# A hybrid encoder layer on one core: the passage to the MLP regrouped by PSUM bank, the residual's squares moved to the units, and the first gate's steps set further apart

## The chip, the core and the metric

The kernel runs on one core of a Trainium2 chip. The metric is the device time of one launch in microseconds (us); several runs are made and their median counts. A profiled execution leaves a trace of every instruction. The engines are named as the profile names them: PE (TensorE matmul), PEld (its weight loads), DVE (VectorE), ACT (ScalarE), POOL (GpSimd) and SP (SyncE, which here only issues DMAs). Each engine works through its own instructions in order and waits on semaphores for the others.

## The reference

One layer of an encoder block on 256 tokens of width 2048, all float32. Three mixers read one projection; the RWKV branch ends in a group norm times a gate. Cut to what matters here:

```
def reference(x, ...):
    mix = hybrid_mixer(_rms_norm(x, norm_mix_pre), w_in, ...)   # 3 branches, gates, w_out
    x = x + _rms_norm(mix, norm_mix_post)
    hdn = jnp.square(jax.nn.relu(_rms_norm(x, norm_mlp_pre) @ w_mlp_up))
    x = x + _rms_norm(hdn @ w_mlp_down, norm_mlp_post)

def rwkv7_time_mix(z, ...):
    ...
    y = ((y - mean) * lax.rsqrt(var + RWKV_GN_EPS) * ln_w + ln_b)
    y = y + jnp.sum(r_h * k_h * r_k, axis=-1, keepdims=True) * v_h
    return y * g                                  # g = sigmoid(gd) @ g_up
```

## The kernel before

Every matrix product runs on PE with operands split in two float32r parts, a high part `hi` (a rounded copy) and a low part `lo = x - hi`. Of weights, which stream from memory in tiles of 128x1024 through three buffers (`raw`, loaded by SP's queue in `wraw`, L145), ACT makes the high part `whi` (L152) and DVE the low part `wlo` (L153). Activations are kept as `pk` tiles of 128x512, the high part in the first half, the low part in the second; `split` (L229 to L234) makes them: ACT writes the high part (L233 with a scale), DVE subtracts (L234). `unit` and `up` then multiply eight `pk` tiles with one weight tile: eight matmuls of 512 columns with `whi` (L168, the last one L176) and eight of 256 columns with `wlo` (L172). A unit is two such halves.

PE's order in the first part of the program (mixers, branches) is written out by hand: `gemm` and `tok` (L214, L198) call `tick` after every few matmuls, which adds their estimated time to a clock, and threads of mixer work (generators that yield "how many us later to go on") put their small steps between the matmuls when their due time has come. `gate_norm` is such a thread, once for each half of the RWKV heads (`hf` 0 and 1). For each of four head pairs `p` it multiplies `y` by the inverse deviation `ri` (DVE, L773), applies weight and bias (ACT, L774), adds the bonus (DVE, L775), computes the gate on PE (L779 and L780, from two small weights `gup` that are loaded one pair ahead by `gup_load`: a POOL memset L751 and two DMAs from ACT's queue, L752 and L753) and multiplies (DVE, L781). The gates' results, like all results of mixer steps, lie in four PSUM banks in turn (`mps`); a bank is free when its reader is done. The `yield` of 7.5 us ahead of the loop and of 2.0 us in it set how far PE's gate matmuls lie apart.

From the last group of the output product on, the order is no longer by hand: a scheduler orders each engine's instructions from its own cost estimates and the order in the code. There the passage to the MLP stands. For each half of the tokens, `tt`, the sum of squares is finished (ACT, L969), `rstd_of` turns it into an inverse root in two POOL instructions on 128x1 (L939, L940), and `add_mixed` (DVE, L956) adds the normed mix to the residual `x1[tt]` (in the trace's rows `x`; in the order's rows `x_1333` for `tt` 0, `x_1334` for `tt` 1). PE transposes it, four blocks of 128x128 into one `mps` bank (L988: blocks `k2` and `k2+1`, both token halves), and the two blocks of a bank are split to the `pk` tiles that feed the MLP's units. ACT and DVE never read one bank at the same time: semaphores keep their reads of a bank apart.

In the first eight units ACT also sums the squares of the residual, 512 columns each time (L1113 in `up`'s `post`); its output tile `junk` is thrown away, only the sum in `ss3` is used, by L1117 to L1120, and from there at the very end. The scheduler may place these squares as early as the residual is there. The residual's copy to memory (`xs`, L1261 and L1262) stands in SP's queue ahead of the next weight loads. The layer ends with `rstd_of` again, once for each token half, and the last additions (L1352).

Of the kernel before, what the change touches and what calls it, by code (L numbers as in the profile page):

```python
# [10 lines left out]
F32 = mybir.dt.float32  # L11
F32R = mybir.dt.float32r
AF = mybir.ActivationFunctionType
ALU = mybir.AluOpType
# [3 lines left out]
T = 256  # L18
D = 2048
# [31 lines left out]
def hybrid_block(ctx, tc, xt, x, gains, params, consts, lora, gup, wst, out):  # L51
    nc = tc.nc
    V, A, G, PE = nc.vector, nc.scalar, nc.gpsimd, nc.tensor
# [21 lines left out]
    def pk():  # L75
        return pkpool.tile([128, 512], F32R, tag="pk", name=nm("pk"), bufs=24)
# [14 lines left out]
    def P(name, i=0, r=slice(0, 128)):  # L91
        return par[r, PC[name] + i:PC[name] + i + 1]
# [134 lines left out]
    def split(src, dst, scale=None):  # L227

        if scale is None:  # L229
            A.activation(dst[:, 0:T], src, AF.Copy)  # L230
            V.tensor_tensor(dst[:, T:], src, dst[:, 0:T].bitcast(F32), ALU.subtract)
        else:
            A.activation(dst[:, 0:T], src, AF.Copy, scale=scale)  # L233
            V.scalar_tensor_tensor(dst[:, T:], src, scale, dst[:, 0:T].bitcast(F32), ALU.mult, ALU.subtract)  # L234
# [64 lines left out]
    for h in range(2):  # L299
        w = {}  # L300
        for k in range(8 * h, 8 * h + 8):
            xsplit(k)
            i = k - 8 * h
            if i in (0, 3, 5):
                j = len(w)
# [36 lines left out]
    for h in range(8):  # L342
        ps = qb[h] if h < 3 else unit(xpk)
# [400 lines left out]
    def gate_norm(hf, y, bon, sy, sz):  # L744
        PR = range(4 * hf, 4 * hf + 4)
        gqs = {}

        def gup_load(p):
            if p in PR:
                gqs[p] = gq = rp.tile([128, 2, 128], F32, tag="gup", name=nm("gup"), bufs=2)  # L750
                G.memset(gq[:, 1, :], 0.0)  # L751
                nc.scalar.dma_start(out=gq[:, 0, :], in_=gup[0:128, 128 * p:128 * p + 128])  # L752
                nc.scalar.dma_start(out=gq[0:32, 1, :], in_=gup[128:160, 128 * p:128 * p + 128])  # L753

        gup_load(PR[0])
        var = rp.tile([128, 4, T], F32, tag="XT", name=nm("gn"), bufs=2)
        ri = rp.tile([128, 4, T], F32, tag="XT", name=nm("gn"), bufs=2)
        sc = rp.tile([128, 4, T], F32, tag="Ti", name=nm("gn"), bufs=1)
        for i, p in enumerate(PR):
            A.activation(sc[:, i, :], y[p], AF.Square)  # L760
            if i % 2:
                yield 1.6
        for i2 in range(2):
            ps = mps()
            for i in range(2):
                PE.matmul(ps[:, i * T:i * T + T], C("bones"), sc[:, 2 * i2 + i, :], start=True, stop=True)
            A.activation(var[:, 2 * i2:2 * i2 + 2], ps.rearrange("p (a b) -> p a b", a=2), AF.Identity, scale=1.0 / 64,
                         bias=cst[:, 1:2])
        yield 2.0
        rsqrt(ri, var, sc)  # L770
        yield 7.5
        for i, p in enumerate(PR):
            V.tensor_tensor(y[p], y[p], ri[:, i, :], ALU.mult)  # L773
            A.activation(y[p], y[p], AF.Identity, scale=P("lnw", p), bias=P("lnb", p))  # L774
            V.tensor_tensor(y[p], y[p], bon[p], ALU.add)  # L775
            gup_load(p + 1)
            gq = gqs[p]
            ps = mps()
            PE.matmul(ps[:, 0:T], gq[:, 0, :], sy, start=True, stop=False)  # L779
            PE.matmul(ps[:, 0:T], gq[:, 1, :], sz, start=False, stop=True)  # L780
            V.tensor_tensor(y[p], ps[:, 0:T], y[p], ALU.mult)  # L781
            yc[p] = y[p]
            yield 2.0
        mark(f"gn{hf}")

    def mixers():
# [41 lines left out]
    for s in ("q", "k"):  # L828
        lst = []
        for h in range(4):  # L830
            ps = unit(upk)
# [11 lines left out]
    for hf in range(2):  # L843
        for s, mo in (("k", MU_K), ("r", MU_R), ("v", MU_V)):
            for p in range(4 * hf, 4 * hf + 4):
                ps = unit(upk)
# [84 lines left out]
    def rstd_of(ss, eps, sums):  # L931

        if sums is None:
            sums = cpool.tile([128, 1], F32, name=nm("ssum"))
            V.tensor_reduce(sums, ss[:, 0:3], AX.X, ALU.add)
            V.tensor_scalar(sums, sums, 1.0 / D, eps, ALU.mult, ALU.add)
            return sums
        r = cpool.tile([128, 1], F32, name=nm("rs"))
        G.tensor_scalar(r, ss[:, 3:4], 1.0 / D, sums, ALU.mult, ALU.add)  # L939
        G.tensor_tensor(r, r, cst[:, 2:3], ALU.pow)  # L940
        return r

    g2, loads = gain(0, [fm().rearrange("p a b -> p (a b)")[:, 0:512] for _ in range(4)])
    x1 = [p2.tile([128, D], F32, tag="x1", name=nm("x1"), bufs=2) for _ in range(2)]
# [7 lines left out]
    def junk():  # L952
        return p2.tile([128, 512], F32, tag="junk", name=nm("junk"), bufs=2)
# [30 lines left out]
    trs = []  # L984
# [6 lines left out]
    for k2 in range(0, KT, 2):  # L991
        while len(trs) < min(k2 // 2 + 4, 8):
            trs.append(mps())
            turned(2 * len(trs) - 2, 0)
        if k2 == 8:
            pend()
        add_mixed(1, 128 * k2, 256)
        turned(k2, 1)
        for i in range(2):
            u = pk()  # L1000
            split(trs[k2 // 2][:, i * T:i * T + T], u, P("g3", k2 + i))
            upk2.append(u)

# [79 lines left out]
    def up(j):  # L1085
# [10 lines left out]
        def post():  # L1096
# [13 lines left out]
            h = hid[j // 2]  # L1110
            A.activation(h[:, 0:4:3] if j % 2 == 0 else h[:, 1:3], t.rearrange("p (s t) -> p s t", s=2), AF.Square)
            if j < 8:
                A.activation(junk(), x1[j % 2][:, 512 * (j // 2):512 * (j // 2) + 512], AF.Square,  # L1113
                             accum_out=ss3[:, j % 2, j // 2:j // 2 + 1])
            if j in (8, 9):
                e = cpool.tile([128, 2], F32, name=nm("eps4"))
# [362 lines left out]
```

## Time and profile before

| | us |
|---|---|
| median of 3 runs | 1534.03 (1532.95 to 1536.06) |
| profiled execution, its own time | 1534.53 |
| its span, first to last instruction | 1532.8 |
| PE busy in it | 1503.2 |
| DVE, ACT, POOL busy | 1192.7, 917.8, 91.0 |

The profiled execution lies 0.50 us above the median. Rows of the timeline read: start, duration, engine, line, operation, output and input tiles, number of instructions merged, and in brackets how long the engine sat idle before and what released it. In rows by stretches of time, each engine's busy time with its instructions in brackets is followed by the granted TensorE clock (1.00 is full), the DMA engines' busy share and GB/s. A matmul's duration contains its passage through the array; the distance from one start to the next is what it costs on a busy PE.

### The profile page before, as it was taken

The page shows a single profiled execution, that of the slowest core. Times are in us where ns is not written, and L with a number is a line of the kernel's source. Part 1 is how long each engine was busy: PE and PEld are TensorE (multiplying, and loading weights), DVE is VectorE, ACT ScalarE, POOL GpSimd, SP SyncE. Part 2 cuts the span into 40 slices and gives each one's busy share as a digit, 9 for nine tenths or more (in the row PEclk, how much of TensorE's full clock was granted, in tenths as well). Part 3 has the DMA queues.
Part 4 walks back from the last instruction along what each step waited for, and adds up shares of the span by engine and source line. Part 5 has one row for each costly group of instructions (what it writes and reads, how often), then busy time and mean ns, then how long its engine had stood idle before and what let it go on. Part 6 is the DMA issues. An engine that isn't in the chain of part 4 may idle for free.

```text
span 1532.8 us, 22383 instructions
## 1 busy us (share of the span) xinstructions
PE 1503.2 (98%) x8294; PEld 1262.6 (82%) x8294; DVE 1192.7 (78%) x1608; ACT 917.8 (60%) x1340; POOL 91.0 (6%) x163
## 2 busy tenths in 40 slices
PE   7999999999999999999999999999999999999997
PEld 6888888888777788778888788888888888888885
DVE  6865567789548789447755868989899999899986
ACT  6664566554546553555444767777667776676753
POOL 0021000000000100000000000000000000000000
PEclk9999999999999999999999999999999999999998
DMA  7555445445534445535695657888888888888974
GB/s 259 192 166 166 164 165 181 165 150 183 182 111 150 165 152 184 175 124 179 208 322 187 231 181 222 249 263 239 262 253 258 242 254 270 249 246 264 260 247 151
DMA packets 105117, 316.88 MB, mean 207 GB/s; under 512 B 10288, under 2 KB 12720, under 8 KB 104624
## 3 DMA queue, kind: packets, MB, share of 16 engines
q1 hardware_dynamic: 93536, 282.76, 54.1%
q0 software_dynamic: 8064, 29.36, 10.3%
q10 hardware_dynamic: 3408, 3.34, 0.6%
q8 instruction: 65, 1.06, 0.3%
q14 instruction: 44, 0.36, 0.1%
HBM read 281.86 MB, written 4.19 MB: 187 GB/s over the span
## 4 chain that ended last, share of the span: by engine, by line
PE 53%; DVE 1%; DMA 1%; ACT 1%; issue 0%; POOL 0%; DVEq 0%; POOLq 0%; ACTq 0%
PE gps L168 14%; PE gps L214 10%; PE gps L172 8%; PE mps L1209 3%; PE mps L1210 3%; PE mps L1211 3%; PE gps L198 3%; PE gps L1211 2%; PE gps L1209 2%; PE gps L1210 2%; PE gps L176 1%; DMA sp<-in_wst_dram 1%; DVE x L1352 0%; DVE wlo L153 0%; ACT junk L1113 0%
## 5 line engine op out<-in xcount | busy, mean ns | idle before, releaser
L153 DVE TENSOR_TENSOR wlo<-raw,whi 128x1024 fp32r<-128x1024 f32 x507 | 616.0, 1222 | 192.2 <-ACT whi L152 174.8
L152 ACT ACTIVATE whi<-raw 128x1024 fp32r<-128x1024 f32 x507 | 533.9, 1057 | 276.0 <-PE gps L214 107.7
L168 PE MATMUL gps<-pk,whi 128*128 128x512 f32 x1301 | 330.9, 393 | 0.1
L214 PE MATMUL gps<-whi,pk 128*128 128x512 f32 x1144 | 291.5, 394 | 0.0
L168 PEld LDWEIGHTS gps<-pk,whi 128*128 128x128 f32 x1301 | 241.1, 188 | 48.4 <-issue 0.9
L214 PEld LDWEIGHTS gps<-whi,pk 128*128 128x128 f32 x1144 | 213.7, 188 | 45.8 <-issue 1.0
L172 PEld LDWEIGHTS gps<-pk,wlo 128*128 128x128 f32 x1391 | 190.1, 190 | 14.6 <-issue 1.2
L172 PE MATMUL gps<-pk,wlo 128*128 128x256 f32 x1391 | 195.8, 283 | 0.0
L214 PE MATMUL gps<-wlo,pk 128*128 128x512 f32 x572 | 157.4, 394 | 0.0
L214 PEld LDWEIGHTS gps<-wlo,pk 128*128 128x128 f32 x572 | 106.9, 188 | 23.2 <-issue 0.7
L1075 DVE TENSOR_TENSOR sp<-raw,sp 128x1024 fp32r<-128x1024 f32 x67 | 81.7, 1220 | 4.8 <-ACT sp L1074 4.6
L1074 ACT ACTIVATE sp<-raw 128x1024 fp32r<-128x1024 f32 x67 | 70.7, 1055 | 14.9 <-PE mps L1211 3.9
L1101 ACT ACTIVATE sp<-gps 128x512 f32<-128x512 f32 x52 | 31.1, 597 | 80.7 <-PE gps L176 80.7
L198 PE MATMUL gps<-whi,pk 128*128 128x512 f32 x264 | 71.9, 393 | 0.0
L1209 PE MATMUL mps<-whi,fm 128*128 128x512 f32 x168 | 66.2, 394 | 0.0
L1210 PE MATMUL mps<-whi,fm 128*128 128x512 f32 x168 | 65.8, 392 | 0.0
L1211 PE MATMUL mps<-wlo,fm 128*128 128x512 f32 x168 | 65.5, 390 | 0.0
L1171 POOL DMA_DIRECT2D raw<-raw x40 | 35.0, 874 | 430.8 <-DVE raw L1168 133.4
L198 PEld LDWEIGHTS gps<-whi,pk 128*128 128x128 f32 x264 | 49.3, 188 | 10.6 <-ACT whi L152 0.2
L1211 PE MATMUL gps<-wlo,fm 128*128 128x512 f32 x126 | 49.3, 391 | 0.4 <-DVE wlo L153 0.4
L1209 PE MATMUL gps<-whi,fm 128*128 128x512 f32 x126 | 49.2, 391 | 0.0
L1168 DVE TENSOR_TENSOR raw<-raw,raw 128x1024 f32<-128x1024 f32 x40 | 48.8, 1219 | 0.4
(342 smaller groups left out, 1961.4 us busy)
## 6 DMA issues: line engine op xcount, KB each, us to landing
raw<-in_wst_dram SPq DMA_DIRECT2D x502, 512.0 KB, 4.4
raw<-raw POOLq DMA_DIRECT2D x40, 512.0 KB, 7.3
sp<-in_wst_dram SPq DMA_DIRECT2D x16, 512.0 KB, 5.6
raw<-sp POOLq DMA_DIRECT2D x8, 512.0 KB, 7.7
sp<-raw POOLq DMA_DIRECT2D x8, 512.0 KB, 6.5
x<-in_x_dram SPq DMA_DIRECT2D x8, 256.0 KB, 6.3
xs<-x SPq DMA_DIRECT2D x2, 1024.0 KB, 4.0
x<-xs SPq DMA_DIRECT2D x4, 512.0 KB, 7.4
```

The source lines that it names most:

```text
L152: A.activation(hi, raw, AF.Copy)
L153: V.tensor_tensor(lo, raw, hi.bitcast(F32), ALU.subtract)
L168: PE.matmul(ps, hi[:, i * 128:i * 128 + 128], pks[i], start=first and i == 0, stop=False)
L172: PE.matmul(ps[:, 0:T], lo[:, i * 128:i * 128 + 128], pks[i][:, 0:T], start=False, stop=False)
L198: PE.matmul(ps[tt], pks[k][:, c:c + 128], w[:, (k - k0) * 512:(k - k0) * 512 + 512], start=k == 0 and part == 0 and w is hl[0], stop=w is ...
L214: PE.matmul(ps[tt], pks[k][:, c:c + 128], w[:, (k - k0) * 512:(k - k0) * 512 + 512], start=k == 0 and part == 0 and w is hl[0], stop=False)
L1074: A.activation(hi, raw, AF.Copy)
L1075: V.tensor_tensor(lo, raw, hi.bitcast(F32), ALU.subtract)
L1168: V.tensor_tensor(x, x, z, ALU.add)
L1209: PE.matmul(Q[f], p, w, start=d == 0 and i == 0, stop=False)
L1210: PE.matmul(Q[f], pl, w, start=False, stop=False)
L1211: PE.matmul(Q[f], p, wl, start=False, stop=d == nd - 1 and i == 1)
```

## The change

Four things. The first half's gate waits 11.5 us instead of 7.5 ahead of its loop and 2.8 instead of 2.0 between pairs. The first of the two small instructions of `rstd_of` moves from POOL to DVE (four instructions in all: two in the passage, two at the end). In the passage the two high parts of a bank are written first and then its two low parts. The residual's squares write their useless output over the unit's own PSUM bank `ps[0]` instead of `junk`, so that each can run only after its unit.

```
-        yield 7.5
+        yield 7.5 if hf else 11.5
         for i, p in enumerate(PR):
             ...
-            yield 2.0
+            yield 2.0 if hf else 2.8
...
-        G.tensor_scalar(r, ss[:, 3:4], 1.0 / D, sums, ALU.mult, ALU.add)
+        V.tensor_scalar(r, ss[:, 3:4], 1.0 / D, sums, ALU.mult, ALU.add)
         G.tensor_tensor(r, r, cst[:, 2:3], ALU.pow)
...
-        for i in range(2):
-            u = pk()
-            split(trs[k2 // 2][:, i * T:i * T + T], u, P("g3", k2 + i))
-            upk2.append(u)
+        src = [trs[k2 // 2][:, i * T:i * T + T] for i in range(2)]
+        us = [pk(), pk()]
+        for i, u in enumerate(us):
+            A.activation(u[:, 0:T], src[i], AF.Copy, scale=P("g3", k2 + i))
+        for i, u in enumerate(us):
+            V.scalar_tensor_tensor(u[:, T:], src[i], P("g3", k2 + i), u[:, 0:T].bitcast(F32), ALU.mult, ALU.subtract)
+        upk2.extend(us)
...
-                A.activation(junk(), x1[j % 2][:, 512 * (j // 2):512 * (j // 2) + 512], AF.Square,
+                A.activation(ps[0], x1[j % 2][:, 512 * (j // 2):512 * (j // 2) + 512], AF.Square,
```

In the changed kernel the lines behind the passage lie three lower (L1113 becomes L1116), and the high and low parts of the passage are L1002 and L1004. The engines' orders differ from before in three places only.

**The first gate.** PE ahead of the third head pair's gate (L779, L780), before; `gps` are the two banks of the weight product that runs meanwhile, L567 and L569 belong to the second half's mixer:

```order
L214 MATMUL gps_4486<-wlo_4558,pk_293 128x512
L214 MATMUL gps_4487<-wlo_4558,pk_293 128x512
L567 MATMUL mps_4616<-zx,lor_4416 128x256
L569 MATMUL mps_4618<-zx,lor_4416 128x256
L214 MATMUL gps_4486<-wlo_4558,pk_294 128x512
L779 MATMUL mps_4643<-zy,gup_4598 128x256
L780 MATMUL mps_4643<-zz,gup_4598 128x256
L214 MATMUL gps_4487<-wlo_4558,pk_294 128x512
```

and now (the weight tiles have other numbers):

```order
L214 MATMUL gps_4487<-whi_4628,pk_298 128x512 x2
L214 MATMUL gps_4486<-wlo_4629,pk_297 128x512
L214 MATMUL gps_4487<-wlo_4629,pk_297 128x512
L214 MATMUL gps_4486<-wlo_4629,pk_298 128x512
L779 MATMUL mps_4690<-zy,gup_4645 128x256
L780 MATMUL mps_4690<-zz,gup_4645 128x256
L214 MATMUL gps_4487<-wlo_4629,pk_298 128x512
```

The third gate now follows 24 more matmuls than before, in the second weight tile after the one with `wlo_4558`; the first gate stands about where the third did, and the fourth 13 matmuls behind the third. ACT's queue at that place, before and now, with the loads of `gup` in it:

```order
L152 ACTIVATE whi_4589<-raw_4587 128x1024
L752 DMA gup_4598<-in_gup_dram 128x128
L753 DMA gup_4598<-in_gup_dram 32x128
L152 ACTIVATE whi_4650<-raw_4648 128x1024
L774 ACTIVATE g_772_3978<-g_772_3978,par 128x256
L752 DMA gup_4639<-in_gup_dram 128x128
L753 DMA gup_4639<-in_gup_dram 32x128
```

```order
L752 DMA gup_4645<-in_gup_dram 128x128
L774 ACTIVATE g_772_3978<-g_772_3978,par 128x256
L576 ACTIVATE lw_4611<-mps_4605,wah 128x256
L577 ACTIVATE tha_4613<-mps_4607,wah 128x256
L578 ACTIVATE lw_4611<-lw_4611,cst 128x256
L774 ACTIVATE g_773_3979<-g_773_3979,par 128x256
L753 DMA gup_4645<-in_gup_dram 32x128
L582 ACTIVATE ep_4615<-cs_4612 128x4x64
L583 ACTIVATE em_4614<-cs_4612 128x256
L587 ACTIVATE g_887_4655<-tha_4613,oka,wah 128x256
L774 ACTIVATE g_774_3980<-g_774_3980,par 128x256
L752 DMA gup_4686<-in_gup_dram 128x128
```

Before, all loads of the third and fourth pair stood ahead of the second L774; now the second load of the third pair stands behind the second L774, and both of the fourth pair behind the third. On DVE one more weight split stands ahead of the first L781.

**The passage.** DVE from the second token half on, before (`pk_7701` and `pk_7704` are the two blocks of the first bank, `mg` the mix):

```order
L956 SCALAR_TENSOR_TENSOR x_1334_7021<-mg_7023,rs_7682,x_1334_7021 128x256 x4
L234 SCALAR_TENSOR_TENSOR pk_7701<-mps_7686,par,pk_7701 128x256
L967 TENSOR_TENSOR mg_7023<-gps_7525,fm_7019 128x512
L956 SCALAR_TENSOR_TENSOR x_1334_7021<-mg_7023,rs_7682,x_1334_7021 128x256
L234 SCALAR_TENSOR_TENSOR pk_7704<-mps_7686,par,pk_7704 128x256
L234 SCALAR_TENSOR_TENSOR pk_7713<-mps_7689,par,pk_7713 128x256
L956 SCALAR_TENSOR_TENSOR x_1334_7021<-mg_7023,rs_7682,x_1334_7021 128x256 x3
```

and now, from the ninth low part on:

```order
L1004 SCALAR_TENSOR_TENSOR pk_7750<-mps_7707,par,pk_7750 128x256
L1004 SCALAR_TENSOR_TENSOR pk_7751<-mps_7707,par,pk_7751 128x256
L956 SCALAR_TENSOR_TENSOR x_1334_7021<-mg_7023,rs_7682,x_1334_7021 128x256 x3
L153 TENSOR_TENSOR wlo_7791<-raw_7788,whi_7790 128x1024
L1004 SCALAR_TENSOR_TENSOR pk_7759<-mps_7719,par,pk_7759 128x256
```

Now L939, L967 and five additions come first, ten low parts follow without a break, then three additions, one weight split and the six remaining low parts. Before, five weight splits (one of them L1075), one sum of weights and the eight small instructions L1117 to L1120 stood among the sixteen low parts. ACT, before:

```order
L1113 ACTIVATE junk_7863,ss_7685<-x_1333_7020 128x512
L233 ACTIVATE pk_7701<-mps_7686,par 128x256
L1113 ACTIVATE junk_7916,ss_7685<-x_1334_7021 128x512
L1113 ACTIVATE junk_7980,ss_7685<-x_1333_7020 128x512
L233 ACTIVATE pk_7704<-mps_7686,par 128x256
L233 ACTIVATE pk_7713<-mps_7689,par 128x256
```

Now the sixteen high parts stand together with one weight tile among them, and each square in its unit, as here in the first one:

```order
L1108 ACTIVATE tmp_7857<-gps_7794 128x256
L152 ACTIVATE whi_7866<-raw_7864 128x1024
L1110 ACTIVATE tmp_7856<-tmp_7856 128x256
L1116 ACTIVATE gps_7794,ss_7685<-x_1333_7020 128x512
L1114 ACTIVATE pk_7861<-tmp_7856 128x2x128
L152 ACTIVATE whi_7888<-raw_7886 128x1024
```

The first load into the space that the residual leaves (`sp`, L1064 in SP's queue) moves 17 places back, and its split (L1074, L1075) out of the passage.

**The end.** DVE's last instructions, before and now (`y_8487` and `y_8479` are the second token half, `pk_13653` and `pk_13645` the gain):

```order
L1341 TENSOR_TENSOR y_8486<-y_8486,pk_13653 128x512
L1352 SCALAR_TENSOR_TENSOR x_2587_13828<-y_8486,rs_13975,x_2587_13828 128x512 x4
L1337 TENSOR_TENSOR y_8487<-y_8487,gps_13923 128x512
L1341 TENSOR_TENSOR y_8487<-y_8487,pk_13653 128x512
L1352 SCALAR_TENSOR_TENSOR x_2588_13829<-y_8487,rs_14008,x_2588_13829 128x512 x4
```

```order
L1355 SCALAR_TENSOR_TENSOR x_2579_13820<-y_8478,rs_13967,x_2579_13820 128x512 x4
L1340 TENSOR_TENSOR y_8479<-y_8479,gps_13915 128x512
L939 TENSOR_SCALAR rs_14000<-ss_7785,ssum_13911 128x1
L1344 TENSOR_TENSOR y_8479<-y_8479,pk_13645 128x512
L1355 SCALAR_TENSOR_TENSOR x_2580_13821<-y_8479,rs_14000,x_2580_13821 128x512 x4
```

L939 has moved here from POOL, ahead of the multiplication by the gain.

## Prediction

> **What bounds the kernel now.** I read the page's head first, then PE's waits, then the clock by stretches.
>
> ```profile
> span 1532.8 us, 22383 instructions
> PE 1503.2 (98%) x8294; PEld 1262.6 (82%) x8294; DVE 1192.7 (78%) x1608; ACT 917.8 (60%) x1340; POOL 91.0 (6%) x163
> PE gps L310 <- ACT whi L152: 8.9, 1, 8.9
> PE mps L988 <- DVE x L956: 2.1, 2, 1.8
> PE mps L779 <- DVE g L781: 2.0, 1, 2.0
> ```
>
> PE bounds: 29.6 us of the span are left to it, and its waits lie at the start (8.9 us, untouched by the change), in the passage (L988) and at one gate matmul (L779). Everything else can only pay where it shortens one of these or the end, after PE's last matmul. But a wait costs more than its length, as the granted clock (first number behind POOL) shows:
>
> ```profile
> 478.00:482.64 4.64, 2.65 (x12) 1.43 (x10) 4.64 (x10) 2.01 (x3) 1.35 (x3) 1.00 0.40 128
> 482.64:486.38 3.74, 3.74 (x10) 2.94 (x10) 3.74 (x7) 2.95 (x7) 0.20 (x1) 0.54 0.70 248
> 841.40:844.98 3.58, 1.44 (x9) 0.84 (x8) 2.86 (x6) 2.02 (x5) 1.41 (x2) 0.97 0.50 195
> 844.98:848.29 3.31, 2.99 (x10) 1.85 (x10) 3.10 (x8) 2.58 (x8) 0.00 (x0) 0.52 0.60 248
> 848.29:857.52 9.23, 7.91 (x47) 6.11 (x47) 8.59 (x23) 7.94 (x21) 0.00 (x0) 1.00 0.67 246
> 890.00:1310.00 420.00, 420.00 (x2170) 360.27 (x2170) 380.64 (x447) 296.12 (x400) 33.01 (x38) 1.00 0.82 244
> ```
>
> After each of the two long waits the clock stands at about half for some 3.4 us. From 890 us on PE is full for 420 us, so what is won earlier is carried to the end.
>
> **The gate.** Its rows, with two full units of matmuls from later on as a measure of the rate, and the loads of `gup`:
>
> ```profile
> 480.15 0.50 PE L214 MATMUL gps<-wlo,pk 128*128 128x512 f32 x1
> 480.37 1.22 DVE L153 TENSOR_TENSOR wlo<-raw,whi 128x1024 fp32r<-128x1024 f32 x1
> 481.84 0.42 DVE L773 TENSOR_TENSOR g<-g,gn 128x256 f32<-128x256 f32 x1
> 482.17 0.42 DVE L781 TENSOR_TENSOR g<-mps,g 128x256 f32<-128x256 f32 x1
> 482.29 0.60 ACT L774 ACTIVATE g<-g,par 128x256 f32<-128x256 f32 x1 [0.20 <-DVE g L773]
> 482.64 0.95 PE L779 MATMUL mps<-zy,gup 128*128 128x256 f32 x2 [1.99 <-DVE g L781]
> 868.53 2.00 PE L168 MATMUL gps<-pk,whi 128*128 128x512 f32 x8
> 870.37 1.12 PE L172 MATMUL gps<-pk,wlo 128*128 128x256 f32 x8
> 871.32 1.78 PE L168 MATMUL gps<-pk,whi 128*128 128x512 f32 x7
> DMA to landing us min/median/max: 1.5/2.2/4.2
> ```
>
> At full clock eight matmuls of 512 columns take 870.37 - 868.53 = 1.84 us, 0.23 each, eight of 256 take 0.95, 0.12 each. The third gate needs the bank that the first one's L781 frees. PE's last matmul ahead of it was issued by 480.15 + 0.23 = 480.38; it stood until 482.64, 2.26 us, and lost 3.74 x (1 - 0.54) = 1.7 us to the clock: 4.0 us in all. Now 24 more matmuls stand ahead of the third gate, so PE comes to it at 480.4 + 24 x 0.23 = 485.9. On DVE one split more (1.22) stands ahead of the first L781: 482.17 + 1.22 + 0.42 = 483.8. The bank is free 2.1 us early: the wait goes, and the clock with it does not fall.
>
> What is late next is a load. The second load of the third gate's weight is queued on ACT behind the second L774, which follows its L773 (now 481.84 + 1.22 = 483.06) by 482.29 - 481.84 = 0.45: issued at 483.5, landed after the median of 2.2 us at 485.7, after the longest at 487.7. It is wanted by L780, two matmuls into the gate, at 486.3. The fourth gate comes 13 matmuls (3.0 us) and a gate (four matmuls, 0.9 us at most) later, at 489.8; its loads stand behind the third L774, behind which I count a split, a scan and three ACT steps after the first L781, about 487.2: landed at 489.4, or 491.4. Both fit at the median and miss by 1.4 to 1.6 us at the worst. Such a miss leaves 2.4 of the 4.0, and if the clock falls once more (1.7) 0.7. Bounds -4.0 to +0.5 (a wait of the old kind and length once more); I take -3.8, since both medians fit.
>
> [...]
>
> **The passage.** Its rows:
>
> ```profile
> 842.91 0.86 POOL L939 TENSOR_SCALAR rs<-ss,ssum 128x1 f32<-128x1 f32 x1 [1.97 <-ACT junk L969]
> 840.98 2.74 DVE L956 SCALAR_TENSOR_TENSOR x<-mg,rs,x 128x512 f32<-128x512 f32 x4 [0.21 <-POOL rs L940]
> 843.85 0.56 POOL L940 TENSOR_TENSOR rs<-rs,cst 128x1 f32<-128x1 f32 x1
> 844.44 1.67 DVE L956 SCALAR_TENSOR_TENSOR x<-mg,rs,x 128x256 f32<-128x256 f32 x4 [0.72 <-POOL rs L940]
> 845.71 0.47 ACT L233 ACTIVATE pk<-mps,par 128x256 fp32r<-128x256 f32 x1 [2.29 <-PE mps L988]
> 849.77 0.87 DVE L234 SCALAR_TENSOR_TENSOR pk<-mps,par,pk 128x256 fp32r<-128x256 f32 x2
> 863.21 0.48 DVE L234 SCALAR_TENSOR_TENSOR pk<-mps,par,pk 128x256 fp32r<-128x256 f32 x1 [0.40 <-ACT pk L233]
> 851.84 2.26 SPq L145 DMA_DIRECT2D raw<-in_wst_dram  x2
> 876.31 1.04 ACT L152 ACTIVATE whi<-raw 128x1024 fp32r<-128x1024 f32 x1
> 879.71 2.00 PE L168 MATMUL gps<-pk,whi 128*128 128x512 f32 x8
> raw<-in_wst_dram SPq DMA_DIRECT2D x502, 512.0 KB, 4.4
> L152 ACT ACTIVATE whi<-raw 128x1024 fp32r<-128x1024 f32 x507 | 533.9, 1057 | 276.0 <-PE gps L214 107.7
> L1113 ACT ACTIVATE junk<-x x8: 616/630/650, 842.7 to 851.9; 128x512 f32<-128x512 f32 x8
> L1113 ACT ACTIVATION_READ_ACCUMULATOR junk<-x x8: 188/200/219, 843.2 to 852.4; 128x1 f32 x8
> ```
>
> L939 on DVE wins nothing here. For the second half it now queues behind the four additions that end at 840.98 + 2.74 = 843.72, takes 0.20 (L936 below), and POOL's L940 starts at 843.9 against 843.85. For the first half a weight split hides it. L967 fills the wait.
>
> From 844.5 DVE runs: five additions 0.40 apart (1.67 less one of 0.48, over three) to 846.5, ten low parts as far apart (0.87 less 0.48) to 850.5, three additions to 851.7, one split (1.2) to 852.9, six low parts, the last begun at 854.9 and done by 855.4; before, that one ended at 863.69. ACT loses eight squares, 8 x (0.63 + 0.20) = 6.6 us, and stays ahead of DVE: from 845.71 sixteen high parts of 0.47 and one weight tile of 1.06 end by 854.3 at the latest. PE then: fifteenth block ready 855.0, eight low matmuls, unit 0 done 856.4; the low weights of unit 1 are split by 852.9 + 2.4 + 1.2 = 856.5; two lots of 0.95, seven matmuls of 0.23 and one more give 860.3; unit 2 takes 2 x (1.84 + 0.95) = 5.6, to 865.9, against 868.53 before. The half clock falls on the first blocks again, since PE still stands until 844.98 and then waits for the first low part: the four matmuls of the first two blocks that fall into it lose 0.23 each, and DVE's pace of 0.40 a block gives about half of the 0.9 back. Term: -2.2. It cannot beat PE's own work after 844.98: three units of 5.6 and 24 transposes, which at a quarter of the columns take no more than 0.12 each, 19.7 of 23.55 us: -3.9 is the one bound. The other: the half clock falls on dense matmuls instead (1.7 of the 2.6 gone) and the next weights come late by as much, +0.8. I take a value near the middle, worked out row by row.
>
> Hidden: the next weight load, issued at 851.84 when a split had freed its buffer, now goes at 852.9; with the median of 4.4 us it is there at 857.3 and wanted at 860.3. If that cover of 3 us went, PE would wait for what is over it. The first `sp` load is moved 17 places back, behind some eight units of work. The squares cost ACT 0.83 in a unit of 5.6 us; no row shows ACT writing to a PSUM bank, but even at twice the price they fit in ACT's idle share (296 of 420 us busy above). Apart from these, SP's and POOL's queues keep their order.
>
> **The end.** Its rows:
>
> ```profile
> 1514.79 0.20 DVE L936 TENSOR_SCALAR ssum<-ssum,eps 128x1 f32<-128x1 f32 x1
> 1524.48 0.69 DVE L1341 TENSOR_TENSOR y<-y,pk 128x512 f32<-128x512 f32 x1 [0.85 <-ACT junk L1338]
> 1524.55 0.76 POOL L939 TENSOR_SCALAR rs<-ss,ssum 128x1 f32<-128x1 f32 x1 [4.29 <-ACT junk L1338]
> 1525.38 0.55 POOL L940 TENSOR_TENSOR rs<-rs,cst 128x1 f32<-128x1 f32 x1
> 1525.97 2.74 DVE L1352 SCALAR_TENSOR_TENSOR x<-y,rs,x 128x512 f32<-128x512 f32 x4 [0.80 <-POOL rs L940]
> ```
>
> Now L939 starts at 1524.48 on DVE, ends at 1524.68, L940 runs from about 1524.75 to 1525.3, L1355 starts at 1525.35 instead of 1525.97; the gain's 0.69 us fit behind L939 just so. Term -0.6, bounds -0.75 and 0. The 7 us longer distances and the bank `ps[0]` held 2 us longer (four banks, a unit each 5.6 us) cost nothing.
>
> **Sum.** -3.8 - 2.2 - 0.6 = -6.6 against the profiled execution's own 1534.53: 1527.9; that execution lies 0.5 above the median, so 1527.4.
>
> **Rivals.** (a) The third or fourth gate now waits for its load. For it: both slacks are under 0.8 us and the longest load took 4.2. Gate term about -0.9, sum -3.7: 1530.3. (b) The half clock behind 482.64 is not the wait's doing and comes anyway. Against it: it follows both long waits at once, and the 420 us without a wait have none. Gate -2.3: 1528.9. [...] (c) The passage gains nothing: the weights or the half clock take back what DVE gives. Sum -4.4: 1529.6. (d) Gate and passage both fall short, (a) with (c): -1.5, 1532.5, no change. (e) Slower: the squares, now between ACT's steps of a unit and ahead of the second weight split, hold up the weights. In a steady unit ACT is through with that weight tile at 876.31 + 1.04 = 877.35 and PE begins on it at 879.71, 2.36 later, so a square of 0.83 fits. The delay would have to reach 3.6 us: then eight units lose 1.2 each, 9.7 with rounding, as much as turns -6.6 into +3. That takes L1116 or L1110 standing 2.7 us for DVE's L1109 behind two weight splits of 1.22. At 3.8 us the sum is 8 x 1.45 - 6.6 = +5: 1539. That a part doesn't do what it says is excluded by the orders: all three places moved.
>
> **How the numbers follow.** Runs of this kernel differ by about 0.2% (3 us), which I take as the bound of no change. Chances: forecast 0.48, (a) 0.13, (b) 0.07, (c) 0.12, (d) 0.13, (e) 0.07. Faster by over 0.2%, below 1531.0: forecast, (b), (c) and nearly two thirds of (a), 0.75; within 0.2%: the rest of (a), and (d), 0.18; slower 0.07. The range reaches from all bounds at their best (-4.0 - 3.9 - 0.75 = -8.7, 1525.3) to just short of (d): 1525.0 to 1532.0.
>
> **What would show it.** Right: no wait of PE for L781 and clock 1.00 from 470 to 500; unit 2's last matmul, counted from the first transpose, 2 us earlier; L1355 0.6 us sooner behind its square. Wrong: a PE wait on `gup` at 485 to 491, a second stretch of half clock near 850, or PE waits on `whi` in the first eight units.

## The result, and the profile after

The changed kernel took 1530.78 us in the median of 14 runs, the kernel before 1534.08 beside it: a ratio of 0.9978, 95% interval 0.997 to 0.9986, so 2.1 to 4.6 us less. The median moved by 3.3 us where 6.6 had been forecast. In the profiled executions the span went from 1532.8 to 1528.7 us, 4.1 less; the account below is made of these two, and then of twelve further traces.

The head of the page after, and the longest waits of PE (us in all, times, longest):

```profile
span 1528.7 us, 22374 instructions
PE 1501.7 (98%) x8294; PEld 1261.3 (83%) x8294; DVE 1192.2 (78%) x1612; ACT 916.2 (60%) x1340; POOL 88.7 (6%) x159
PE gps L310 <- ACT whi L152: 9.0, 1, 9.0
PE mps L988 <- DVE x L956: 2.2, 2, 1.9
PE mps L567 <- DVE SC L622: 1.1, 1, 1.1
```

The wait for L781 is gone, and a wait of 1.1 us for L622 that was not there before stands third.

**The gate.** The changed kernel by stretches (clock behind POOL's busy time), then PE's rows of the third and fourth gate and of the next head pair's scores:

```profile
470.00:500.00 30.00, 28.93 (x143) 22.84 (x141) 25.50 (x39) 17.04 (x24) 3.80 (x10) 1.00 0.49 161
485.43 0.59 PE L779 MATMUL mps<-zy,gup 128*128 128x256 f32 x2
489.40 0.59 PE L779 MATMUL mps<-zy,gup 128*128 128x256 f32 x2
493.12 1.16 PE L613 MATMUL mps<-Bt,At 64*128 64x128 f32 x16
499.60 0.48 PE L567 MATMUL mps<-zx,lor 64*128 64x256 f32 x1 [1.07 <-DVE SC L622]
```

The same two rows of before:

```profile
497.38 1.16 PE L613 MATMUL mps<-Bt,At 64*128 64x128 f32 x16
502.70 0.48 PE L567 MATMUL mps<-zx,lor 64*128 64x256 f32 x1
```

Up to L613 PE is 4.26 us ahead. Of that it had 0.49 at L766 already (461.32 against 461.81), before anything of the change runs: 3.77 are the gate's, against a forecast of 3.8, and the clock stays at 1.00. But 6 us later, at L567, the lead is 3.10. PE stood there for DVE's L622, and DVE's, ACT's and SP's rows of the changed kernel say why:

```profile
483.54 1.21 DVE L153 TENSOR_TENSOR wlo<-raw,whi 128x1024 fp32r<-128x1024 f32 x1
484.68 0.68 DVE L579 TENSOR_TENSOR_SCAN cs<-con,lw 128x256 f32<-128x256 f32 x1
...
489.88 0.41 DVE L781 TENSOR_TENSOR g<-mps,g 128x256 f32<-128x256 f32 x1
490.21 1.21 DVE L153 TENSOR_TENSOR wlo<-raw,whi 128x1024 fp32r<-128x1024 f32 x1
491.45 0.33 SPq L145 DMA_DIRECT2D raw<-in_wst_dram  x1
496.62 1.06 ACT L152 ACTIVATE whi<-raw 128x1024 fp32r<-128x1024 f32 x1 [5.22 <-DMA raw<-in_wst_dram]
497.71 1.23 DVE L153 TENSOR_TENSOR wlo<-raw,whi 128x1024 fp32r<-128x1024 f32 x1 [3.36 <-ACT whi L152]
498.85 1.28 DVE L622 TENSOR_TENSOR SC<-mps,con 128x512 f32<-128x512 f32 x2
```

From 484.68 to 490.21 DVE does gate and score steps and no weight split. A split is what frees a buffer for the next load: the six loads between 480 and 495 us each go out within 0.1 us behind the end of a split, this one at 491.45 behind the split that ends at 491.42. It lands some 5 us later, ACT has waited 5.22 us for it, and DVE's split of it stands ahead of L622. What PE had won, DVE and the load had not.

**The passage.** PE's first and second transposes and the first lot of the fourth unit in the changed kernel; then ACT and DVE in the middle of it; then the clock by stretches of 3.4 us:

```profile
838.74 1.29 PE L988 MATMUL mps<-ident,x 128*128 128x128 f32 x8 [0.28 <-DVE x L956]
841.91 1.62 PE L988 MATMUL mps<-ident,x 128*128 128x128 f32 x8 [1.88 <-DVE x L956]
864.28 2.00 PE L168 MATMUL gps<-pk,whi 128*128 128x512 f32 x8
849.28 1.06 ACT L152 ACTIVATE whi<-raw 128x1024 fp32r<-128x1024 f32 x1 [2.44 <-PE gps L168]
850.33 2.30 ACT L1002 ACTIVATE pk<-mps,par 128x256 fp32r<-128x256 f32 x6
851.20 2.44 DVE L1004 SCALAR_TENSOR_TENSOR pk<-mps,par,pk 128x256 fp32r<-128x256 f32 x6 [1.13 <-ACT pk L1002]
840.14:843.55 3.41, 1.62 (x8) 0.80 (x8) 3.34 (x9) 1.16 (x4) 0.55 (x1) 1.00 0.66 269
843.55:846.96 3.41, 3.07 (x11) 2.47 (x11) 3.11 (x9) 2.70 (x8) 0.00 (x0) 0.50 0.09 38
846.96:850.38 3.42, 3.42 (x25) 3.01 (x24) 3.11 (x6) 1.10 (x2) 0.00 (x0) 1.00 0.18 77
```

From the first transposes to the fourth unit it takes 864.28 - 838.74 = 25.54 us; before it was 868.53 - 841.88 = 26.65. That is 1.1 less, where 2.2 had been forecast. The low clock lies on the first blocks' matmuls, and ACT's weight tile, which stands ahead of the last six high parts, waits 2.44 us for PE to let go of an older tile.

**The end**, changed kernel:

```profile
1520.40 0.19 ACT L1341 ACTIVATION_READ_ACCUMULATOR junk<-y 128x1 f32 x1
1520.62 0.21 DVE L939 TENSOR_SCALAR rs<-ss,ssum 128x1 f32<-128x1 f32 x1 [0.85 <-ACT junk L1341]
1520.75 0.68 DVE L1344 TENSOR_TENSOR y<-y,pk 128x512 f32<-128x512 f32 x1
1520.91 0.93 POOL L940 TENSOR_TENSOR rs<-rs,cst 128x1 f32<-128x1 f32 x1 [4.51 <-DVE rs L939]
1521.87 2.74 DVE L1355 SCALAR_TENSOR_TENSOR x<-y,rs,x 128x512 f32<-128x512 f32 x4 [0.44 <-POOL rs L940]
```

L1355 starts 1.28 us behind the end of its square (1520.59), against 1.52 before: 0.24 won, not 0.6. L939 costs what was reckoned, but L940, which took 0.55, now takes 0.93 (for both token halves), with DVE's L1344 running beside it. As the first token half's L1355 comes sooner by the same amount and DVE is the bound from there, the stretch from PE's last matmul to the end of the span shrinks by 0.5 in all (11.5 to 11.0).

### The profile page after: what moved, and what is told of

The parts are those of the page before. It is cut to its first block, busy times and chain, and to the rows that moved or that the text cites. A ratio compares the mean times of both kernels' runs of the same rounds, so it can differ in the third digit from the quotient of the medians.

```text
span 1528.7 us, 22374 instructions
## 1 busy us (share of the span) xinstructions
PE 1501.7 (98%) x8294; PEld 1261.3 (83%) x8294; DVE 1192.2 (78%) x1612; ACT 916.2 (60%) x1340; POOL 88.7 (6%) x159
## 3 DMA queue, kind: packets, MB, share of 16 engines
q0 software_dynamic: 8064, 29.36, 10.2%
## 4 chain that ended last, share of the span: by engine, by line
PE 52%; DVE 1%; DMA 1%; issue 1%; ACT 0%; POOL 0%; POOLq 0%; DVEq 0%; ACTq 0%
PE gps L168 14%; PE gps L214 10%; PE gps L172 8%; PE mps L1214 3%; PE mps L1212 3%; PE mps L1213 3%; PE gps L198 3%; PE gps L1214 2%; PE gps L1212 2%; PE gps L1213 2%; PE gps L176 1%; DMA sp<-in_wst_dram 1%; DMA raw<-in_wst_dram 1%; DVE wlo L153 0%; DVE raw L1171 0%
## 5 line engine op out<-in xcount | busy, mean ns | idle before, releaser
L152 ACT ACTIVATE whi<-raw 128x1024 fp32r<-128x1024 f32 x507 | 533.7, 1057 | 274.8 <-PE gps L214 97.9
L168 PE MATMUL gps<-pk,whi 128*128 128x512 f32 x1301 | 331.6, 394 | 0.4 <-DVE pk L1004 0.4
L168 PEld LDWEIGHTS gps<-pk,whi 128*128 128x128 f32 x1301 | 241.5, 189 | 48.9 <-issue 1.2
L1214 PE MATMUL mps<-wlo,fm 128*128 128x512 f32 x168 | 65.7, 391 | 0.3 <-DVE wlo L153 0.3
L1214 PE MATMUL gps<-wlo,fm 128*128 128x512 f32 x126 | 49.3, 391 | 0.4 <-DVE wlo L153 0.4
```

The source lines that it names most:

```text
L152: A.activation(hi, raw, AF.Copy)
L168: PE.matmul(ps, hi[:, i * 128:i * 128 + 128], pks[i], start=first and i == 0, stop=False)
L1214: PE.matmul(Q[f], p, wl, start=False, stop=d == nd - 1 and i == 1)
```

## The experiments

Four stretches are measured in each trace: from the gate's L766 to the L567 behind L613; from the passage's first transposes to the fourth unit (found as the lot of eight L168 that starts 50.28 or 50.29 us ahead of the first matmul on an `fm` tile, in every trace); from there to PE's end; and from PE's end to the end of the span. "Low" is the number of 3.4 us periods of half clock in the passage. The stretches are read from one trace a kernel. The difference is that of the medians of the runs made side by side, with the interval of the ratio; with 10 to 14 runs a kernel (5 of the one with the gain ahead) it resolves about 0.1%. Two kernels were run once only.

| kernel | gate | passage | low | units | end | against before, us (ratio's interval) |
|---|---|---|---|---|---|---|
| before | 40.89 | 26.65 | 1 | 652.8 | 11.5 | |
| before once more | 40.91 | 26.69 | 1 | 652.1 | 11.4 | one run |
| changed | 38.28 | 25.54 | 1 | 653.4 | 11.0 | -3.3 (0.9970 to 0.9986) |
| gate alone | 38.50 | 27.39 | 2 | 653.8 | 11.5 | -2.8 (0.9972 to 0.9990) |
| squares alone | 40.90 | 25.32 | 1 | 654.6 | 11.5 | -0.8 (0.9988 to 1.0006) |
| regrouping alone | 40.88 | 27.27 | 1 | 653.6 | 11.5 | -0.2 (0.9990 to 1.0011) |
| both of the passage | 40.89 | 27.00 | 2 | 652.5 | 11.5 | -0.5 (0.9986 to 1.0005) |
| changed, PE kept busy | 38.68 | 24.11 | 0 | 654.5 | 11.1 | -3.8 (0.9969 to 0.9989) |
| the same, not regrouped | 38.81 | 25.44 | 0 | 654.1 | 11.0 | one run |
| changed, distances 6.5 | 39.67 | 25.68 | 1 | 653.2 | 11.0 | -3.3 (0.9973 to 0.9996) |
| changed, distances 5.0 | 37.26 | 25.49 | 1 | 652.7 | 11.0 | -4.7 (0.9965 to 0.9984) |
| changed, gain ahead | 38.40 | 25.69 | 1 | 654.7 | 10.2 | -5.9 (0.9949 to 0.9977) |
| distances 5.0 and gain | 37.22 | 25.62 | 1 | 655.2 | 10.2 | -3.7 (0.9967 to 0.9984) |
| the two and PE kept busy | 37.27 | 24.11 | 0 | 656.8 | 10.2 | -4.0 (0.9964 to 0.9983) |

**Is the wait at L567 the gate's doing?** The kernel before with nothing but

```
-        yield 7.5
+        yield 7.5 if hf else 11.5
-            yield 2.0
+            yield 2.0 if hf else 2.8
```

> The kernel before with the longer distances in the first half's gate alone. Theory: in the changed kernel the gate's steps gave all that was forecast (PE came to the scores' L613 3.8 us sooner than before, once the 0.5 us by which the whole execution ran ahead is taken off), but 1.1 us was given back 6 us later, where PE waited 1.07 us at L567 for DVE's L622, which stood behind a weight split whose weights had been loaded late, because DVE ran thirteen gate and score steps in a row without a split. So alone: L613 3.8 sooner, again a wait of about 1.1 at L567, clock 1.00 from 470 to 500, sum -2.7 us. Rival: the wait at L567 was an accident of that execution or came from the other parts: no wait at L567, sum -3.8 us. Second rival: the half clock at 482 was not the doing of PE's wait and comes again: sum -1 us or less.

L766 to L613 took 493.22 - 461.45 = 31.77 us, in the changed kernel 31.80, before 35.57: 3.80 sooner. And the wait is there again:

```profile
499.95 0.48 PE L567 MATMUL mps<-zx,lor 64*128 64x256 f32 x1 [1.33 <-DVE SC L622]
```

The theory holds for the gate, and both rivals fall. Five traces have these distances; their gate stretch takes 38.28 to 38.81 us, and each waits at L567, for 0.66 to 1.33 us. The sum of -2.8 hides something that no theory had: the passage, which this kernel doesn't touch, took 27.39 us, 0.7 more than before. Its clock stayed low for two periods instead of one:

```profile
840.91:844.32 3.41, 2.09 (x10) 1.09 (x10) 2.69 (x8) 1.62 (x6) 0.66 (x2) 1.00 0.75 308
844.32:847.73 3.41, 2.60 (x9) 2.05 (x9) 3.36 (x10) 3.41 (x12) 0.00 (x0) 0.50 0.04 14
847.73:851.15 3.42, 3.42 (x13) 2.72 (x12) 3.42 (x6) 2.71 (x8) 0.00 (x0) 0.50 0.99 363
```

**Which half of the passage's change pays?** First only the squares go to `ps[0]`:

```
-                A.activation(junk(), x1[j % 2][...], AF.Square,
+                A.activation(ps[0], x1[j % 2][...], AF.Square,
```

> The kernel before with the residual's squares written to the units' bank alone, so that they leave the passage; each block's high part is still followed by its low part. Measured from the first transposes of the passage to the first matmul of the fourth unit: 26.65 us before, 25.54 in the changed kernel. Theory: the passage's gain (1.1) came from both parts, and most of it from the squares leaving ACT: some 25.9 here, sum -0.7 us. Rival: the regrouping carries it, the squares only filled ACT's idle time: 26.6, sum 0.

Then only the regrouping (`split` replaced by two high parts and two low parts), with the squares left on `junk`:

> The kernel before with the regrouping of the passage alone (two high parts, then two low parts); the residual's squares stay in the passage on ACT. Same stretch as for the squares alone. Theory: four squares stand between the eighth and the ninth high part on ACT, 0.8 us each, so the ninth block is late and the stretch is 27 us or more, sum 0 to +1 us. Rival: the regrouping carries the gain: 25.6, sum -1.1 us.

Then both:

> The kernel before with both parts of the passage (regrouping and squares) and nothing else. Theory: the stretch from the first transposes to the fourth unit takes 25.5 us as in the changed kernel, 1.1 less than before, since ACT's weight tile ahead of the last six high parts waits some 2.4 us for PE to let go of an older tile; sum -1.1 us. The forecast had -2.2 (24.4 us). Rival: the 25.5 holds only together with the gate or the step L939 on DVE, and alone it is 26 or more, sum -0.5 us or less.

The squares alone brought the passage to 25.32 us, more than their theory gave and as far as both parts together in the changed kernel. The regrouping alone made it longer (27.27), as its theory had it: four squares keep ACT busy from 848.51 to 851.12 between the eighth and the ninth high part. Both without the rest of the change took 27.00, the number of the rival. But this figure contains a second low period, so it neither stands against the 25.54 of the changed kernel nor shows that L939 or the gate is needed for it. None of the three can be told from the kernel before by its time. By these three runs regrouping is worth nothing, and how much of that is the clock is left open.

**The same with the clock held up.** The changed kernel with twelve transposes more, whose results are overwritten, where PE waits for the second token half:

```
+        if k2 == 0:
+            for n in range(12):
+                PE.transpose(trs[n % 4][:, 128:256], x1[0][:, 128 * n:128 * n + 128], C("ident"))
         if k2 == 8:
             pend()
```

> The changed kernel with twelve transposes more, whose result is overwritten, in PE's wait for the second half of the residual at the passage, so that PE works through the wait. Theory: the clock falls to half for 3.4 us where PE has been busy for too small a share of the 3.4 us before, so now it stays at 1.00 from the passage's first transposes on; the blocks' matmuls then take 0.23 instead of twice that, the eighth high matmul comes 1.4 us sooner and with it the weight tile that ACT waits for: the stretch from the first transposes to the fourth unit falls from 25.5 to about 24 us, sum -1.5 us against the changed kernel. Rival: the low clock has another cause (the program's phase, the load at the passage) and comes in any case: 25.5 to 27 us, sum 0 to +1.5 us. Second rival: the clock stays up, but DVE's pace of 0.40 a block and ACT's weight tile set the time anyway: sum -0.3 us.

And that kernel with `split` for each block again:

> The changed kernel with the twelve transposes more but without the regrouping: each block's high part is followed by its low part, as in the kernel before; the squares stay out of the passage. With the clock at 1.00 throughout, the stretch from the first transposes to the fourth unit (24.1 us with the regrouping) shows what the regrouping is worth. Theory: nothing or less, as 25.3 us with the squares alone against 25.5 with both speaks for: 23.8 to 24.3 us. Rival: the low clock hid what it is worth: 25 us or more.

```profile
839.40:842.80 3.40, 2.57 (x22) 2.33 (x22) 3.33 (x7) 1.00 (x3) 0.55 (x1) 1.00 0.47 189
842.80:846.20 3.40, 3.05 (x19) 1.93 (x18) 3.40 (x10) 3.11 (x9) 0.00 (x0) 1.00 0.53 214
863.54 2.00 PE L168 MATMUL gps<-pk,whi 128*128 128x512 f32 x8
```

These are rows of the regrouped one. Between its first lot of L168 and the lot behind the second transposes stand four matmuls and six transposes; here, and then in the changed kernel with its low clock, these lots start at:

```profile
844.59 0.73 PE L168 MATMUL gps<-pk,whi 128*128 128x512 f32 x2 [0.35 <-DVE pk L1007]
846.20 0.94 PE L168 MATMUL gps<-pk,whi 128*128 128x512 f32 x3
```

```profile
843.89 1.22 PE L168 MATMUL gps<-pk,whi 128*128 128x512 f32 x2 [0.35 <-DVE pk L1004]
846.90 0.98 PE L168 MATMUL gps<-pk,whi 128*128 128x512 f32 x3
```

That is 1.61 us against 3.01, a loss of 1.40 to the clock. With useless work in the gap the clock doesn't fall (no low period in the table's three kernels with PE kept busy, one or two in the other eleven), and the passage takes 24.11 us (863.54 - 839.43; the last kernel of the table repeats it): 1.43 less than in the changed kernel. The five traces of the regrouped passage with the squares moved and one low period take 25.49 to 25.69. It is the low clock that comes from the gap, as the first theory said, and it had cost 1.4 us. Without regrouping the passage takes 25.44 with the clock at 1.00 and 25.32 with it low: there the clock doesn't matter, because PE isn't the pace. ACT's rows of that kernel show what is:

```profile
850.04 0.84 ACT L233 ACTIVATE pk<-mps,par 128x256 fp32r<-128x256 f32 x2 [1.08 <-DVE pk L234]
851.96 0.84 ACT L233 ACTIVATE pk<-mps,par 128x256 fp32r<-128x256 f32 x2 [1.08 <-DVE pk L234]
```

Each pair of high parts waits for DVE's low part of the bank. So the rival of this last run is right: the low clock hid what the regrouping is worth. With the clock up it is 25.44 - 24.11 = 1.33 us; with the clock low PE itself becomes the pace and takes it back. The two passages that are not regrouped are one trace each, and the 25.32 comes from a kernel with the old gate and L939 on POOL.

**Can the wait at L567 be taken away?** The distance of 2.8 between pairs of the first half became 6.5, then 5.0:

> The changed kernel with distances of 6.5 instead of 2.8 between the gates of the first half, which spreads their rows on DVE: a weight split stands after five gate and score steps instead of after thirteen. Theory: the weights' loads are issued sooner, the split ahead of DVE's L622 is done sooner, and PE's wait of 1.07 us at L567 goes: sum -1.1 us against the changed kernel. Rival: the wait is set by the chain of the scores (L613 to L622) itself, or the last gate's L781 now stands in its way: the wait stays at about 1 us or grows, sum 0 to +1 us.

> The changed kernel with distances of 5.0 instead of 2.8: a split stands after nine steps instead of thirteen, and only three splits instead of four stand between that run of steps and L622. Theory (loads wait for splits): the wait at L567 shrinks to less than 0.5 us, sum -0.6 to -1.1 us. Rival (the wait is set by the scores' own chain): unchanged at 1.1 us.

With 6.5 the wait only moved: the third gate now comes behind the scores and needs a bank that L622 frees. It waits 2.11 us, and the clock falls behind that wait too, to 0.50 for 3.40 us:

```profile
500.04 0.70 PE L779 MATMUL mps<-zy,gup 128*128 128x256 f32 x2 [2.11 <-DVE SC L622]
497.90:501.30 3.40, 1.29 (x7) 1.12 (x7) 3.14 (x5) 0.71 (x2) 0.07 (x1) 1.00 0.66 199
501.30:504.70 3.40, 3.40 (x11) 1.81 (x9) 2.36 (x4) 1.06 (x2) 0.13 (x1) 0.50 0.37 134
```

The gate stretch is 1.4 us longer than in the changed kernel: here the rival's outcome came, by a wait in another place than it named. (This execution was 2 us late at L766 already: it has a low clock at 177.04 us that no other trace has.) With 5.0 the wait at L567 is gone, and a shorter one at L619 (0.91 us, for DVE's L781) stands in its place; the stretch is 37.26 us, 1.0 shorter, as the theory had it. No load is waited for there: ACT's L152 waits for PE instead (2.6 us). That fits loads waiting for splits, but the edit moves gates and splits together, so it doesn't single out the load.

**Why does L940 take 0.93 us?** The changed kernel with the last gain written to a tile of its own, ahead of the square:

```
+            yg = junk() if g == 3 else yv
+            if g == 3:
+                V.tensor_tensor(yg, yv, g4[g], ALU.mult)
             A.activation(junk(), yv, AF.Square, accum_out=ss4[:, tt, g:g + 1])
...
                 r4 = rstd_of(ss4[:, tt, :], None, sum4[tt])
-                gained()
...
-                    V.scalar_tensor_tensor(x1[tt][:, cs], ys[tt][:, cs], r4, x1[tt][:, cs], ...)
+                    V.scalar_tensor_tensor(x1[tt][:, cs], ys[tt][:, cs] if c < 1536 else yg, r4, x1[tt][:, cs], ...)
```

> The changed kernel with the last gain multiplication (L1344 there) written to a tile of its own ahead of the square, where DVE stood idle for 0.85 us, instead of beside POOL's L940. Theory: POOL's L940 took 0.93 us in the changed kernel instead of 0.55 because DVE ran L1344 from the same memory beside it; alone it takes 0.55 again, and the last L1355 starts 0.8 us behind its square's end instead of 1.28: sum -0.4 to -0.5 us at the end. Rival: L940 is slow there for another reason (it comes right behind DVE's L939): it stays 0.93, the start comes 1.2 us behind, sum -0.1 us.

```profile
1521.58 0.69 DVE L1343 TENSOR_TENSOR junk<-y,pk 128x512 f32<-128x512 f32 x1
1522.12 0.19 ACT L1344 ACTIVATION_READ_ACCUMULATOR junk<-y 128x1 f32 x1
1522.63 0.55 POOL L940 TENSOR_TENSOR rs<-rs,cst 128x1 f32<-128x1 f32 x1 [4.45 <-DVE rs L939]
1523.21 2.08 DVE L1357 SCALAR_TENSOR_TENSOR x<-y,rs,x 128x512 f32<-128x512 f32 x3 [0.66 <-POOL rs L940]
```

With nothing beside it L940 takes 0.55 again, still right behind DVE's L939: the rival falls. L1357 starts 0.90 us behind its square's end instead of 1.28, and with both token halves the end is 0.85 us shorter (10.18 against 11.03). That is more than the 0.4 to 0.5 of the theory, which counted one half. By the medians this kernel is 2.6 us ahead of the changed one (-5.9 against -3.3, the first from 5 runs); that much the trace does not show. What runs on DVE beside it matters: in the changed kernel L940 took 0.93 beside L1344, whose two inputs are SBUF tiles, and 0.56 and 0.55 in the passage beside L967, whose first input is a PSUM bank. No run shows whether it is the inputs that make the difference.

**Do the gains add?** Distances of 5.0 with the gain ahead, and then the twelve transposes as well:

> The changed kernel with both edits that paid: distances of 5.0 in the first half's gate, and the last gain multiplication ahead of the square. Theory: the edits lie 1000 us apart and add: from the gate's L766 to the next but one step's L567 37.3 us as with the distances alone (38.3 in the changed kernel), and from PE's last matmul to the end of the last square 2.5 us as with the gain alone (2.9), with the last L1357 0.9 behind it (1.28): sum -1.0 - 0.8 = -1.8 us against the changed kernel, about -5 against the kernel before. Rival: what PE wins is lost again in the long stretch of full units between 870 and 1520 us, which took from 652.5 to 654.7 us in the runs so far: sum -1 us or less.

> As the last, with the twelve transposes more in the passage's wait besides. Theory: the passage gives 1.4 us more (24.1 us from the first transposes to the fourth unit, clock 1.00 throughout), and all three add: -3.2 us against the changed kernel, about -6.5 against the kernel before. Rival: units that begin sooner only meet the weights' splits sooner: with the transposes alone the stretch of full units took 654.5 us instead of 653.4, so the sum is -2 us, no better than without them.

The edited stretches add exactly (37.22 and 10.2 in the one, 37.27, 24.11 and 10.2 in the other). The sum doesn't come: -3.7 and -4.0 us against the kernel before, no better than each edit alone. The stretch of units took 655.2 and 656.8 us, so the rivals were right that the time is lost there. In the last kernel PE waits in it:

```profile
PE gps L1217 <- DVE wlo L153: 2.4, 3, 1.1
PE gps L168 <- DVE junk L1222: 0.9, 1, 0.9
```

Where in the units the time goes can be read by lining up the starts of PE's matmuls, counted from the fourth unit. In all fourteen traces the first 1720 matmuls start at the same times to 0.002 us, 330 us long. Only behind 1190 us do the traces part, by single steps of up to 1.3 us, most of them at or just behind matmuls that use the low part of a weight (L1211, L1214, L1217). The last kernel has three such steps of over 1 us, at 1364.7, 1425.5 and 1427.6 us. So a lead is not eaten up as the units begin.

**What one kernel repeats to.** The kernel before once more:

> The kernel before once more, for what two executions of one kernel differ by in each stretch. Theory: the gate and the end repeat to 0.1 us, the passage takes 26.65 us or, where the low clock lasts for two of its periods of 3.4 us instead of one, 27.4 as with the gate's distances alone; the stretch of full units differs by up to 2 us. Rival: every stretch repeats to 0.1 us, so that what differed between the kernels there comes from their edits.

Gate, passage and end repeated to 0.1 us, the units came out 0.7 apart (652.8 and 652.1): the theory, though here the low clock lasted one period both times. Most of that is one step of 0.58 us in the first of the two, at L1211 at 1338.4 us. At L766 the two executions already stood 0.36 us apart (461.81 and 461.45).

Whether any of these versions beats the changed kernel is not settled: the one with the gain ahead has the lowest median (1528.96 us, 5 runs), but its interval, 0.9949 to 0.9977, overlaps that of the changed kernel.

## Why the prediction was partly right

The forecast was 1527.4 us; 1530.78 lies in its range. The side was right and each of the three places gained, but about half of the size did not come. That 1530.78 lies nearest to rival (a)'s 1530.3 is chance: PE waits for no load of `gup`. The 4.1 us between the profiled executions are: 0.49 that the second one had ahead of any change (two executions of the kernel before differ by 0.36 there), gate 2.61, passage 1.11 and 0.04 between the two, end 0.48, and 0.63 lost again in the units.

- **Gate, -3.8 forecast, -3.77 measured at L613, -2.6 kept.** That the wait goes and takes the half clock with it held. The loads of `gup` fitted: no PE wait names them, so rival (a) did not come. The step that failed is "What is late next is a load". It looked for the next late thing among the gate's own instructions; the next late thing was a weight split on DVE, whose load could not start while DVE did thirteen other steps in a row. One row of DVE's order behind the gate would have asked the question. Rival (b) is excluded: no half clock between 470 and 500 us in the changed kernel nor with the gate alone. That splits free the buffers is seen; that the late load alone makes the wait at L567 is argued, since no run moved it by itself.
- **Passage, -2.2 forecast, -1.11 measured.** The row-by-row count gave 865.9 - 841.88 = 24.0 us; with the clock held up the passage took 24.11. So the steps of DVE were counted right (ACT's weight tile waits 1.70 us for PE there too, but DVE's additions and split cover it), and the mis-sized one is "the four matmuls of the first two blocks that fall into it lose 0.23 each", of which half was to come back. Those four lost 0.9 as counted, but the six transposes between them lost 0.5 more, and nothing of the 1.4 came back, since PE and not DVE set the pace there. That ACT "stays ahead of DVE" failed with it: the weight tile's wait of 2.44 us for PE was not in the count. Rival (c), half-way true, is the nearer description.
- **End, -0.6 forecast, -0.48 measured**, -0.24 of it behind the last square. "L940 runs from about 1524.75 to 1525.3" took its duration from a row in which DVE was idle beside it (L1341 ended at 1525.17); in its new place it took 0.93. The other 0.24 comes from the first token half, which the forecast had not counted.
- **"What is won earlier is carried to the end"** failed in part. It held to 0.002 us for the first 330 us of the units, where every trace runs alike; the 0.63 were lost behind 1190 us, where PE meets weights' low parts that come late. The row that it rested on shows PE busy, not that nothing else is close behind. In fourteen traces the five whose fourth unit starts after 868 us took 652.1 to 653.6 us for the units, the nine that start earlier 652.7 to 656.8. That is a tendency, with the kernel with distances of 5.0 (start at 864.0, 652.7 us) against it. Where the early start was largest, PE's waits for DVE's splits are seen: PE stood 3.35 us in these units, against 0.84 before. Which of the steps come in an execution, and why, stays open; the two executions of the kernel before differ by one too.
- **The squares in the units** cost nothing: no PE wait on `whi` in the first eight units, and the fourth unit begins 50.28 us ahead of the first `fm` matmul with them as without (50.29 before). Rival (e) did not come.

## What to carry to other kernels

When a wait of the bounding engine goes, follow the lead to the next place where that engine meets each other engine, and ask whether that one has become earlier too: here DVE and a load had not, and 1.2 of 3.8 us went 6 us later. A gap on PE can cost its length and, as here, a low clock behind it (1.4 us in the passage), and filling it with work that is thrown away is a cheap way to learn how much of a stage the clock was. Two edits may each look worthless because a third thing sets the pace: test them again with that taken away.

## What the runs showed of the hardware

In these traces the clock falls on a grid. From slices of 0.2 us, in the kernel before and in that with distances of 6.5, the moment can be worked out (0.87 means that the last 0.26 of the slice were at half):

```profile
482.80:483.00 0.20, 0.20 (x2) 0.17 (x3) 0.20 (x2) 0.20 (x2) 0.00 (x0) 0.87 0.21 41
844.60:844.80 0.20, 0.00 (x0) 0.00 (x0) 0.20 (x1) 0.00 (x0) 0.00 (x0) 0.90 1.01 410
501.20:501.40 0.20, 0.20 (x2) 0.16 (x1) 0.20 (x1) 0.00 (x0) 0.17 (x1) 0.76 1.15 410
849.40:849.60 0.20, 0.20 (x1) 0.12 (x1) 0.20 (x2) 0.20 (x2) 0.00 (x0) 0.66 0.01 0
```

The falls are 844.76 - 482.95 = 361.81 us apart in the one, 849.46 - 501.30 = 348.16 in the other: 106 and 102 times 3.413, the length of one low stretch (3.41 in the rows by stretches above). In all eleven traces with more than one fall, that behind PE's end counted, the distances are such multiples to 0.01 us, up to 1525.30 - 177.04 = 395 times 3.413. In the gate and the passage the low clock lasted 3.41 or 6.83 us.

In the period of the grid ahead of a fall in the gate or the passage PE had been busy for 1.29 to 2.09 us of 3.41 (rows above have 1.29, 1.62 and 2.09). The gaps were of some 2 us (PE waits of 1.99, 1.88 and 2.11 in the rows shown). In these two stretches the clock never fell behind a period with more: 2.27 us is the least that was followed by a full clock (with the gain ahead, 838.19 to 841.60), and with PE kept busy the period of the grid, worked back from this trace's fall at 1520.33, had 2.37 (841.07 to 844.49). But busy time alone does not decide. With the squares alone PE was busy for 2.04 us from 1428.30 to 1431.71, a period of that trace's grid, and the clock stayed up. With distances of 6.5 it fell at 177.04 behind a period in which PE was busy throughout, more than half of it with matmuls on 4 rows (L439, L447). What decides between one period and two was not found either: with the gate alone PE was busy for 2.60 us of the first low period and the clock stayed down, in the changed kernel for 3.07 and it came back, but with both parts of the passage alone for 3.05 and it stayed down.
